# Three PSUM banks for the input projection during the recurrence of a hybrid decoder layer

## The chip, the cores and the metric

The kernel runs on one core of a Trainium2 chip. The metric is the device time of one execution in microseconds, as the median of several runs. Each kernel is also executed once under the hardware profiler; that execution has a time of its own, and the trace covers its span from the first to the last instruction.

The engines are TensorE (PE in the profile; its weight loads PEld), VectorE (DVE), ScalarE (ACT), GpSimd (POOL) and SyncE (SP), which issues the DMAs. TensorE writes its products to PSUM, eight banks of 128 x 512 float32; here ScalarE and VectorE read them out, and a bank can take a new product when the last reader of the old one is done.

## What is computed

One decoder layer for 1024 tokens of width 1024, float32. The part this change touches is the projection of the normed input and the RWKV-7 recurrence fed by it:

```
u = rmsnorm(h, mix_pre_norm)
z = u @ w_in                      # attention q,k,v | r,k,v,w,a,g of the recurrence | gates
# per head, 64 x 64 state, for every token t:
sa    = state @ a_t               # a_t = -kk
state = state * w_t + sa b_t^T + v_t k_t^T
y_t   = state @ r_t
```

Behind it come the normalisation of y, a causal attention over three dilated groups, a gated merge of both branches, an output projection, a squared-ReLU MLP with 4096 hidden columns, and a gated embedding, each with an RMSNorm.

## The kernel before

Every product of dense weights is done in three float32r products of a high and a low part (mm3, lines 289 to 297): L292 high by high, L294 and L296 the mixed ones. So a half of a projection (zhalf, line 348: one 128-column weight tile by 512 tokens) is 24 matmuls of 128x512 into one bank named z. Each weight tile is loaded raw (wr), split by ScalarE into its high part (wh) and by GpSimd into its low part (wl). One weight tile serves two halves, so two z banks in turn.

The recurrence is done in chunks of 64 tokens, for four units w of two heads each (128 channels). For a unit the steps are:

- elementwise (line 596): decays, the key norm (hs, rn, bc), then AR and BK, the scaled keys and receivers; then the products A of BK and AR, four tokens' chunks at a time, masked by VectorE into the tile TM.
- invert (690): the inverse of a triangular matrix per chunk. VectorE does 31 pairs of operations on xy and pt; they are put into its gaps. Then 32x32 transposes on VectorE (TN<-xy, TM<-xy) and two sets of 32 small products on TensorE, tq and tr, whose results ScalarE copies to TQ and TN.
- fold_v (747) and fold (772): vt and kv bring the values in; bt and at are transposes of BK and AR, fq, kx and wr are products that fold the inverse into one matrix and one vector per chunk.
- scan (828): 14 states in a row; each is one product q on TensorE and one operation AR<-q on VectorE.
- read_out (840) and post (862): y, its norm (hv, yt on TensorE; sq, yc, vc, rb on ScalarE and VectorE).

Between these small products TensorE works on halves of z: of the units' r, k and v, of the attention's q, k, v, and of the gates (16 tiles that no step waits for soon, which fill).

The program has no order that stands in the text. A planner (class Order, line 136) runs generators at build time: the chains of the recurrence when their modelled operands are ready, else the next matmul of a dense half. It records all instructions of an engine in the order in which it came to them, and each engine executes in that order. The planner has modelled durations of every engine, and for the banks of the chains a time until which each is busy: chain_bank (308) takes the bank of its tags that is free earliest and lets other work go ahead until then. For a bank of z it has no such time. What the chip waits for are the semaphores between writer and readers of a tile, and of a bank.

The eight banks carry the tags z0, z1, s0 to s3, m0, m1. z takes its banks in turn by a counter (zbank, 341). The chains before the change: m0 and m1 for most steps; s2 and s3 for A besides, and for y; s0 and s1 for at, kx and q.

Of the kernel before, what the change touches and what calls it, by code (L numbers as in the profile page):

```python
# [26 lines left out]
NU = RW // 128  # L27
# [217 lines left out]
def layer(ctx: ExitStack, tc: tile.TileContext, x, pT, wz, wup, w_out, wff1, w_ff2, w_ple, w_pleg,  # L245
# [26 lines left out]
    done = set()  # L272

    def mm(out_, a, b, us, start=True, stop=True):
        PE.matmul(out_, a, b, start=start, stop=stop)  # L275
        m = math.prod(a.shape[1:])
        sch.turn("full" if a.shape[0] > 64 and m > 64 else (a.shape[0], m))
        sch.t = max(sch.t, sch.written.since(a, None) - 0.1, sch.written.since(b, None) - 0.1) + us
        sch.written.put(out_, sch.t, None)
        sch.dep = sch.t  # L280

    def tr(out_, a, us, idn=None):
        PE.transpose(out_, a, ident if idn is None else idn)  # L283
        sch.turn("full" if a.shape[0] > 64 else a.shape[0])
        sch.t = max(sch.t, sch.written.since(a, None) - 0.1) + us
        sch.written.put(out_, sch.t, None)
        sch.dep = sch.t
# [20 lines left out]
    def chain_bank(shape, name, tags=("m0", "m1")):  # L308
        tag = sch.first(tags)
        yield from sch.free(tag)  # L310
        return psum.tile(shape, F32, name=name, tag=tag), tag
# [28 lines left out]

    def zbank():
        tags = ("z0", "z1", "s0")
        if ("X", 0) in done and ("P", NU - 1, 1) not in done:
            tags = tags[0:2]
        zn[0] += 1
        return psum.tile([128, 512], F32, name="z", tag=tags[zn[0] % len(tags)])

# [6 lines left out]
    with tc.tile_pool(name="xin", bufs=1) as xp:  # L354
# [19 lines left out]
        def keep_warm(n):  # L374
            keep = zbank()[:, 0:128]
            for i in range(n):
                mm(keep, one, one, 0.107)
# [3 lines left out]
        for b, c in enumerate((slice(0, 512), slice(512, 1024))):  # L381
            ps = psum.tile([128, 512], F32, name="gb", tag=f"s{b + 2}")
# [28 lines left out]
        def z_quarter(n, q):  # L411
            h, ts = q // 2, slice((q % 2) * 256, (q % 2) * 256 + 256)
            if q % 2 == 0:
                zl[h].append(psum.tile([128, 512], F32, name="z", tag="s3") if h and n else zbank())
            hi, lo = wl[n]
            now(mm3(zl[h][n][:, ts], [(hi[:, k * 128:k * 128 + 128], lo[:, k * 128:k * 128 + 128],
                                       uT[0][h][:, k, ts], uT[1][h][:, k, ts]) for k in range(KT)]))
# [63 lines left out]
    def add_z(wi, evac, gate=None):  # L481
        def body(hi, lo):
            for h in range(2):
                ps = zbank()
                yield from zhalf(ps, hi, lo, h)
                evac(h, ps)
        sch.add(body, lambda: wload(wz[wi]), gate)
# [25 lines left out]
    for h in range(2):  # L513
        for n, t in ((0, xw), (1, xg)):
            ps = zl[h][n]
# [256 lines left out]
    def fold(w):  # L772
        d = U[w]
        AR, BK, TM, TN, UV, wc = (d[n] for n in ("AR", "BK", "TM", "TN", "UV", "wc"))
        for b in range(4):
            ps, tag = yield from chain_bank([128, 4, 128], "bt")
            for i in range(4):
                tr(ps[:, i, :], BK[:, 4 * b + i, :], 0.11)
            S.activation(TM[:, 4 * b:4 * b + 4, 0], ps.rearrange("p c (h k) -> p c h k", h=2), AF.Copy)
            sch.hold(tag)  # L780
        t0 = sch.dep
        for b in range(2):
            ps, tag = yield from chain_bank([128, 4, 128], "at", ("s0", "s1"))
            for i in range(4):
                c = 8 * b + 2 * i
                tr(ps[:, i, :], AR[:, 0, c:c + 2].rearrange("p c t -> p (c t)"), 0.11)
            for i in range(2):
                S.activation(BK[0:64, 8 * b + i:8 * b + 8:2, :], ps[64 * i:64 * i + 64], AF.Copy)
            sch.hold(tag)
        yield sch.until(t0)  # L790
        for g in range(4):
            ps, tag = yield from chain_bank([128, 4, 128], "fq")
            for i in range(4):
                for h in range(2):
                    mm(ps[64 * h:64 * h + 64, i, :], TN[:, 2 * (4 * g + i) + h, :],
                       TM[0:64, 4 * g + i, :, h], 0.095)
            ps = ps.rearrange("p c (x t) -> p c x t", x=2)
            S.activation(TM[0:64, 4 * g:4 * g + 4, :, 0], ps[0:64], AF.Copy)
            V.tensor_copy(TM[0:64, 4 * g:4 * g + 4, :, 1], ps[64:128])
            sch.hold(tag)  # L800
        yield sch.until(sch.dep)
        for g in range(2):
            cg = slice(8 * g, 8 * g + 8)
            ps, tag = yield from chain_bank([128, 8, 64], "kx", ("s0", "s1"))
            for i in range(8):
                for h in range(2):
                    hp = slice(64 * h, 64 * h + 64)
                    mm(ps[hp, i, :], TM[:, 8 * g + i, 0, h], UV[:, 8 * g + i, hp], 0.06)
            V.tensor_tensor(AR[:, 0, cg], ps, wc[:, cg, None].to_broadcast([128, 8, 64]), OP.mult)
            sch.hold(tag)  # L810
        for g in range(4):
            cg = slice(4 * g, 4 * g + 4)
            ps, tag = yield from chain_bank([128, 4, 128], "wr")
            for i in range(4):
                for h in range(2):
                    hp = slice(64 * h, 64 * h + 64)
                    mm(ps[hp, i, :], BK[0:64, 4 * g + i, hp], TM[0:64, 4 * g + i, :, h], 0.095)
            for h in range(2):
                V.scalar_tensor_tensor(TM[:, cg, 0, h], ps[:, :, 0:64], hb[h],
                                       ident[:, None, 64 * h:64 * h + 64].to_broadcast([128, 4, 64]),  # L820
                                       op0=OP.mult, op1=OP.add)
            V.tensor_tensor(AR[:, 1, cg], ps[:, :, 64:128], AR[:, 1, cg], OP.add)
            sch.hold(tag)
        done.add(("F", w))
# [3 lines left out]
    def scan(w):  # L828
        d = U[w]
        AR, TM, wc = d["AR"], d["TM"], d["wc"]  # L830
        for c in range(1, NCH - 1):
            if c % 8 == 1:
                qb, tag = yield from chain_bank([128, 8, 64], "q", ("s0", "s1"))
            q = qb[:, (c - 1) % 8, :]
            mm(q, TM[:, c, 0].rearrange("p h k -> p (h k)"), AR[:, 0, c - 1], 0.113)
            V.scalar_tensor_tensor(AR[:, 0, c], q, wc[:, c:c + 1], AR[:, 0, c], op0=OP.mult, op1=OP.add)
            sch.hold(tag)
            yield None
# [73 lines left out]
    def rwkv():  # L912
        for w in range(NU):
            yield from fold_v(w)
            yield from wait(lambda: ("T", w) in done)
            yield from fold(w)
            yield from scan(w)
            yield from read_out(w)
# [752 lines left out]
    P = {}  # L1671
# [265 lines left out]
```

## Time and profile before

| | us |
|---|---|
| median of 3 runs | 1775.32 |
| lowest and highest run | 1775.20, 1776.92 |
| profiled execution | 1773.19 |
| its span, first to last instruction | 1771.4 |
| TensorE, time with a matmul under way | 1743.8 |
| VectorE busy | 1017.1 |
| ScalarE busy | 732.3 |
| GpSimd busy | 670.5 |

The stages in the trace: the load and norm of the input to about 57 us, the recurrence with its projections from there to about 490, the attention with the rest of the projections to about 824, then merge, output projection, MLP and embedding to the end.

How the lines are read. A timeline row has the start in us, the length, the engine, the line, the operation, what is written and read with its shapes, and how many instructions the row merges; in brackets how long the engine was idle before, and who ended that. Most operations of VectorE, ScalarE and GpSimd are recorded by one helper and show as L113, small products as L275, transposes on TensorE as L283, DMAs as L132; there the tile names tell them apart. A float32 product that is not float32r shows as two matmuls. A row of busy time by stage has the stretch, its length, then for PE, PEld, DVE, ACT and POOL the busy time and the number of instructions, then the granted TensorE clock as a share, the DMA engines' busy share and GB/s. A row of waits has the engine and its product, who ended the wait, the total in us, the number of times and the longest.

### The profile page before, as it was taken

To read this page: it belongs to the slowest core of one execution; us is meant where nothing else is said; L and a number is where in the kernel's file an instruction comes from. 1 tells how busy PE (TensorE), PEld (TensorE's weight loads), DVE (VectorE), ACT (ScalarE), POOL (GpSimd) and SP (SyncE) were. 2 spreads that over 40 slices of the span, in tenths; PEclk is the share of its full clock that TensorE was granted. 3 is DMA by queue.
4 is the path that set the end of the run, shared out by engine and by line. 5 is a ranking of instruction groups with operands and counts; after the bars stand their busy time and mean duration, and the time that the engine had idled before them with its cause. 6 is when DMAs were issued, how large, how long until landed. Compare 5 with 4: busy or idle time off the path is not lost.

```text
span 1771.4 us, 25935 instructions
## 1 busy us (share of the span) xinstructions
PE 1743.8 (98%) x10192; PEld 1423.4 (80%) x10192; DVE 1017.1 (57%) x1834; ACT 732.3 (41%) x1315; POOL 670.5 (38%) x423
## 2 busy tenths in 40 slices
PE   9999989999999999999999999999999999999998
PEld 8787877878877777778888878888788888888887
DVE  6289777776534233353735466665666566556643
ACT  5824343432344343542434434343334334333454
POOL 1344131231232323332230266666665566652311
PEclk9999999999999999999999999999999999999999
DMA  4621121212332222333524132332232232305611
GB/s 163 211 95 37 49 78 47 98 43 96 86 134 84 60 60 72 110 111 135 201 96 139 64 113 95 94 115 87 92 118 91 84 95 90 123 9 179 214 48 48
DMA packets 67132, 175.51 MB, mean 99 GB/s; under 512 B 7745, under 2 KB 8129, under 8 KB 66498
## 3 DMA queue, kind: packets, MB, share of 16 engines
q1 hardware_dynamic: 67010, 173.86, 29.6%
q8 instruction: 80, 1.31, 0.3%
q14 instruction: 42, 0.34, 0.1%
HBM read 125.20 MB, written 41.94 MB: 94 GB/s over the span
## 4 chain that ended last, share of the span: by engine, by line
PE 82%; DVE 5%; DMA 5%; ACT 3%; POOL 2%; issue 2%; SPq 0%; DVEq 0%; ACTq 0%; POOLq 0%
PE z L294 18%; PE z L296 18%; PE z L292 18%; PE bk L292 6%; PE bk L294 5%; PE bk L296 5%; PE sc L275 1%; DVE xy L113 1%; PE y L275 1%; PE po L275 1%; PE pt L283 1%; PE A L275 1%; PE wr L275 1%; PE fq L275 1%; POOL wl L113 1%
## 5 line engine op out<-in xcount | busy, mean ns | idle before, releaser
L113 POOL TENSOR_TENSOR wl<-wr,wh 128x1024 fp32r<-128x1024 f32 (+1 forms) x87 | 208.0, 2392 | 431.4 <-ACT wh L113 412.2
L113 DVE TENSOR_TENSOR tot<-tot,bk 128x512 f32<-128x512 f32 x420 | 272.7, 682 | 129.9 <-PE bk L296 129.7
L292 PE MATMUL z<-uh,wh 128*128 128x512 f32 (+1 forms) x800 | 312.3, 390 | 5.5 <-ACT part L113 3.0
L296 PE MATMUL z<-uh,wl 128*128 128x512 f32 (+1 forms) x800 | 312.6, 391 | 2.7 <-POOL wl L113 2.7
L294 PE MATMUL z<-ul,wh 128*128 128x512 f32 (+1 forms) x800 | 313.6, 392 | 1.3 <-DVE ul L113 1.3
L292 PE MATMUL z<-f,wh 128*128 128x512 f32 x496 | 193.2, 389 | 0.3 <-ACT f L113 0.3
L294 PE MATMUL z<-f,wh 128*128 128x512 f32 x496 | 193.1, 389 | 0.2 <-DVE f L113 0.2
L296 PE MATMUL z<-f,wl 128*128 128x512 f32 x496 | 193.0, 389 | 0.0
L292 PEld LDWEIGHTS z<-uh,wh 128*128 128x128 f32 x800 | 151.1, 189 | 36.2 <-ACT part L113 3.5
L296 PEld LDWEIGHTS z<-uh,wl 128*128 128x128 f32 x800 | 151.0, 189 | 34.1 <-POOL wl L113 4.0
L294 PEld LDWEIGHTS z<-ul,wh 128*128 128x128 f32 x800 | 151.2, 189 | 32.3 <-issue 3.6
L292 PE MATMUL bk<-duo 128*128 128x512 f32 x420 | 164.3, 391 | 4.0 <-DVE tot L113 3.9
L294 PE MATMUL bk<-duo 128*128 128x512 f32 x420 | 163.5, 389 | 0.0
L296 PE MATMUL bk<-duo 128*128 128x512 f32 x420 | 163.5, 389 | 0.0
L113 ACT ACTIVATE wh<-wr 128x1024 fp32r<-128x1024 f32 (+1 forms) x87 | 90.3, 1038 | 119.0 <-PE z L294 89.8
L113 POOL TENSOR_TENSOR duo<-w2r,duo 128x512 fp32r<-128x512 f32 x45 | 66.7, 1483 | 166.0 <-ACT duo L113 166.0
L113 POOL TENSOR_TENSOR duo<-ws,duo 128x512 fp32r<-128x512 f32 x60 | 81.0, 1350 | 122.3 <-ACT duo L113 119.0
L292 PEld LDWEIGHTS z<-f,wh 128*128 128x128 f32 x496 | 93.1, 188 | 20.0 <-ACT f L113 0.5
L294 PEld LDWEIGHTS z<-f,wh 128*128 128x128 f32 x496 | 93.1, 188 | 19.8 <-DVE f L113 0.5
L296 PEld LDWEIGHTS z<-f,wl 128*128 128x128 f32 x496 | 93.1, 188 | 19.2
L292 PEld LDWEIGHTS bk<-duo 128*128 128x128 f32 x420 | 78.8, 188 | 23.7 <-DVE tot L113 7.0
L296 PEld LDWEIGHTS bk<-duo 128*128 128x128 f32 x420 | 78.8, 188 | 16.4
(312 smaller groups left out, 3203.5 us busy)
## 6 DMA issues: line engine op xcount, KB each, us to landing
wr<-in_wz_dram SPq DMA_DIRECT2D x48, 512.0 KB, 3.7
wr<-in_wff_dram SPq DMA_DIRECT2D x31, 512.0 KB, 3.6
w2r<-in_w_ff_dram SPq DMA_DIRECT2D x30, 512.0 KB, 4.2
xt<-in_x_dram SPq DMA_DIRECT2D x16, 512.0 KB, 4.3
gscr<-gst SPq DMA_DIRECT2D x32, 256.0 KB, 2.0
g<-gscr SPq DMA_DIRECT2D x16, 512.0 KB, 4.2
wpg<-pkg SPq DMA_DIRECT2D x16, 512.0 KB, 6.7
sw<-qk SPq DMA_DIRECT2D x48, 128.0 KB, 2.3
```

The lines of the kernel that those rows point to most:

```text
L113: return f(*a, **kw)
L275: PE.matmul(out_, a, b, start=start, stop=stop)
L283: PE.transpose(out_, a, ident if idn is None else idn)
L292: PE.matmul(ps, ah, bh, start=start and i == 0, stop=False, skip_group_check=not start)
L294: PE.matmul(ps, ah, bl, start=False, stop=False, skip_group_check=not start)
L296: PE.matmul(ps, al, bh, start=False, stop=i == n - 1, skip_group_check=not start)
```

## The change

z takes three banks (z0, z1, s0) at all times; before, it took only two of them from the start of the recurrence until its last unit was done. In exchange the chains give up s0. The transposes at and the products kx may use s1, m0 or m1, whichever is free earliest; the states q of the scan use s1 alone.

```
     def zbank():
         tags = ("z0", "z1", "s0")
-        if ("X", 0) in done and ("P", NU - 1, 1) not in done:
-            tags = tags[0:2]
         zn[0] += 1
         return psum.tile([128, 512], F32, name="z", tag=tags[zn[0] % len(tags)])
...
-            ps, tag = yield from chain_bank([128, 4, 128], "at", ("s0", "s1"))
+            ps, tag = yield from chain_bank([128, 4, 128], "at", ("s1", "m0", "m1"))
...
-            ps, tag = yield from chain_bank([128, 8, 64], "kx", ("s0", "s1"))
+            ps, tag = yield from chain_bank([128, 8, 64], "kx", ("s1", "m0", "m1"))
...
-                qb, tag = yield from chain_bank([128, 8, 64], "q", ("s0", "s1"))
+                qb, tag = yield from chain_bank([128, 8, 64], "q", ("s1",))
```

The planner sees other banks for the chains, and from the first folding on, at about 182 us of the trace before, it comes to another order, on all engines, until the end of the attention. The matmuls are the same 8637 in both programs.

The largest move that the prediction speaks of is at the second unit's inverse (w = 1). On TensorE there, the products tq and tr before:

```order
L275 MATMUL A<-AR,BK 128x128 x8
L275 MATMUL tq<-TN,TM 32x32 x32
L294 MATMUL z<-ul_128,wh 128x512
...
L275 MATMUL A<-AR,BK 128x128 x8
...
L275 MATMUL A<-AR,BK 128x128 x8
...
L275 MATMUL tr<-TQ,TM 32x32 x32
L296 MATMUL z<-uh_127,wl 128x512
L283 MATMUL bt<-cs,BK 128x128 x4
```

and with the change:

```order
L275 MATMUL tq<-TN,TM 32x32 x32
L292 MATMUL z<-uh_127,wh 128x512
L275 MATMUL hv<-cs,sq 128x2 x4
L294 MATMUL z<-ul_129,wh 128x512
L296 MATMUL z<-uh_127,wl 128x512
L292 MATMUL z<-uh_127,wh 128x512
L275 MATMUL tr<-TQ,TM 32x32 x16
L294 MATMUL z<-ul_129,wh 128x512
L275 MATMUL tr<-TQ,TM 32x32 x16
```

The products A of the third unit, which stood before, between and behind, now come after bt and at; four z matmuls and one hv are left between tq and the first tr, where 16 z and two groups of A stood. Ahead of tq there are now 15 z matmuls, two half groups of bc and kv since vt; before there were 42 z besides bc, kv, hv, two groups of A and yt.

On VectorE, what stands between the two transposes that tq and tr read, before:

```order
L113 STREAM_TRANSPOSE TN<-xy 32x32x32
L113 TENSOR_TENSOR TM<-A,cs 128x8x64 x2
L113 SCALAR_TENSOR_TENSOR yc<-yc,pr,yt 128x512
L113 TENSOR_TENSOR yc<-yc,bv 128x512
L113 SCALAR_TENSOR_TENSOR og<-yc,pr,og 128x512
L113 STREAM_TRANSPOSE TM<-xy 32x32x16x2
```

and with the change:

```order
L113 STREAM_TRANSPOSE TN<-xy 32x32x32
L113 COPY UV<-kv 64x8x64
L113 SCALAR_TENSOR_TENSOR kk<-k,pr,bc 128x512
L113 SCALAR_TENSOR_TENSOR AR<-kk,Ep 128x16x63
L113 TENSOR_SCALAR AR<-kk 128x16
L113 TENSOR_TENSOR BK<-BK,En 128x16x64
L113 STREAM_TRANSPOSE TM<-xy 32x32x16x2
L113 STREAM_TRANSPOSE TN<-xy 32x32x32
L113 TENSOR_TENSOR BK<-BK,kk 128x16x64
L113 RECIPROCAL vc<-vc 128x8
```

The third unit's elementwise steps, which were done before the first transpose, now stand between the two, and the reciprocal of the first unit's norm stands behind both.

On ScalarE, a little earlier, the high part wh of a weight has moved ahead of the third unit's key norm. Before:

```order
L113 ACTIVATE BK<-a,oka,pr 128x16x64
L113 ACT_TABLE_LOAD
L113 ACTIVATE rn<-rn 128x16
L113 ACTIVATE kk<-rn 128x512 x2
L113 ACT_TABLE_LOAD
L113 ACTIVATE En<-Ep 128x1024
L113 ACTIVATE Ep<-Ep 128x1024
L113 ACTIVATE wh<-wr 128x1024
```

and with the change:

```order
L113 ACTIVATE BK<-a,oka,pr 128x16x64
L113 ACTIVATE wh<-wr 128x1024
L113 ACT_TABLE_LOAD
L113 ACTIVATE rn<-rn 128x16
L113 ACTIVATE kk<-rn 128x512 x2
L113 ACT_TABLE_LOAD
L113 ACTIVATE En<-Ep 128x1024
L113 ACTIVATE Ep<-Ep 128x1024
```

GpSimd's low part of the same weight moves with it. Behind the products tq and tr, ScalarE's copies of tr (TN<-tr) now stand after vc and rb of the first unit's norm, and rb reads the reciprocal named above.

## The prediction

> **What bounds the kernel now.** I read the page first, then busy time by stage, then TensorE's waits, then the instructions in order of time at the two places the waits name.
>
> ```profile
> span 1771.4 us, 25935 instructions
> PE 1743.8 (98%) x10192; PEld 1423.4 (80%) x10192; DVE 1017.1 (57%) x1834; ACT 732.3 (41%) x1315; POOL 670.5 (38%) x423
> ```
>
> TensorE is busy for 98% of the span, and the change neither adds nor removes a matmul. What it can win is idle time of TensorE, in the stages where it acts: from 146 us to the early attention at 560.
>
> ```profile
> 146.00:152.00 6.00, 2.69 (x15) 1.99 (x16) 4.80 (x12) 5.94 (x9) 2.81 (x2) 1.00 0.02 5
> 152.00:155.40 3.40, 3.40 (x10) 2.63 (x9) 3.40 (x3) 1.47 (x2) 3.40 (x5) 0.50 0.00 0
> ...
> 182.00:262.00 80.00, 75.38 (x708) 61.14 (x704) 60.54 (x126) 29.60 (x43) 20.10 (x15) 1.00 0.19 63
> 262.00:330.00 68.00, 67.06 (x742) 54.80 (x740) 49.73 (x98) 21.66 (x36) 12.72 (x13) 1.00 0.22 75
> 330.00:490.00 160.00, 158.88 (x1489) 130.95 (x1488) 106.83 (x202) 60.13 (x90) 42.41 (x25) 1.00 0.25 80
> 490.00:560.00 70.00, 67.92 (x488) 52.45 (x486) 32.06 (x97) 32.77 (x84) 18.46 (x8) 1.00 0.33 110
> ```
>
> Length minus the first busy column is TensorE's idle time: 3.31, 0, 4.62, 0.94, 1.12 and 2.08 us, 12.1 in all (from 155.4 to 182 it never idled). The second row also ran at a granted clock of 0.50. More than these 12.1 us and the slow clock cannot be won. Who ended the waits between 140 and 490 us:
>
> ```profile
> PE z L292 <- ACT part L113: 3.0, 1, 3.0
> PE z L296 <- POOL wl L113: 1.5, 1, 1.5
> PE A L275 <- ACT yc L113: 1.2, 1, 1.2
> PE z L292 <- ACT gst L113: 1.0, 1, 1.0
> ```
>
> The first and the last are z products that wait until ScalarE has emptied an old z bank: two waits, 4.0 us. These a third bank can remove.
>
> **Place one, 148 to 164 us (the same order before and after).**
>
> ```profile
> 146.28 1.18 PE L283 MATMUL bc<-cs,kk 128*128 128x128 f32 x8 [0.36 <-ACT kk L113]
> ...
> 147.99 0.40 PE L296 MATMUL z<-uh,wl 128*128 128x512 f32 x1
> ...
> 150.68 0.68 ACT L113 ACTIVATE part<-z,pr 128x512 f32<-128x512 f32 x1
> ...
> 151.42 0.50 PE L292 MATMUL z<-uh,wh 128*128 128x512 f32 x1 [3.03 <-ACT part L113]
> ...
> 156.10 0.39 PE L294 MATMUL z<-ul,wh 128*128 128x512 f32 x1
> 156.32 0.39 PE L296 MATMUL z<-uh,wl 128*128 128x512 f32 x1
> ...
> 163.37 0.39 PE L292 MATMUL z<-uh,wh 128*128 128x512 f32 x1
> 163.69 2.06 PE L275 MATMUL A<-AR,BK 64*128 64x128 f32 x32
> ```
>
> The z half that starts at 151.42 is the 13th z tile of the kernel's counter; with two tags it takes the bank of the 11th, whose second copy (part) ends at about 151.3. With three it takes the bank of the 10th, emptied a projection earlier. So the wait goes: 151.42 - 147.99 = 3.43, less the normal step of 0.23 (156.10 to 156.32), is 3.20 us. The 13 matmuls from 151.42 to 156.10 took 4.68 against 13 x 0.23 = 2.99: the slow clock cost another 1.7. TensorE would reach the decay products A at 163.69 - 3.20 - 1.7 = 158.8.
>
> But A reads BK, and VectorE is the one late next:
>
> ```profile
> 151.50 2.50 POOL L113 TENSOR_TENSOR AR<-r,Ep 128x1024 f32<-128x1024 f32 x1
> 151.79 2.35 DVE L113 TENSOR_TENSOR xy<-xy,pt 64x112 f32<-64x112 f32 x1
> 154.06 1.39 DVE L113 SCALAR_TENSOR_TENSOR kk<-k,pr,bc 128x512 f32<-128x512 f32 x2
> 155.48 2.01 DVE L113 SCALAR_TENSOR_TENSOR AR<-kk,Ep 128x1008 f32<-128x1008 f32 x1
> 157.41 2.37 DVE L113 TENSOR_SCALAR AR<-kk 128x16 f32<-128x16 f32 x1
> 159.69 1.21 DVE L113 TENSOR_TENSOR BK<-BK,En 128x1024 f32<-128x1024 f32 x1
> 161.76 1.21 DVE L113 TENSOR_TENSOR BK<-BK,kk 128x1024 f32<-128x1024 f32 x1
> ```
>
> VectorE runs without a gap from 151.79 to 162.97 and waits for nothing of TensorE's there (its last input of TensorE's, bc, ended at 147.5). BK is done at 161.76 + 1.21 = 163.0 whether or not z waited. So A starts at 163.0 instead of 163.69: the stall moves from the z bank to A, about 4.2 us long, and the gain is 0.7. After an idle stretch of 3.03 us TensorE ran 3.4 us at half clock; if 4.2 us of idling does the same, 1.7 are lost again behind A. Bounds -0.7 and +1.0; the 1.0 + 1.5 us of idling around 228 us did not slow the clock, so I take the middle, +0.2. [...]
>
> **Place two, the second unit's inverse (in the trace 218 to 275 us).** Two waits go: z for gst (1.0), and wl (1.5), since the split of that weight (wh on ScalarE) now stands ahead of the third unit's key norm instead of behind its exponentials. The planner also moves the third unit's A and the first unit's yt behind the inverse, so the wait A <- yc (1.2) goes. Together the idle time there is the 4.62 above. What comes instead: the second inverse's products tq and tr now stand close together. Between them stood 16 z and two A, now 4 z and one hv (four products).
>
> ```profile
> 239.77 2.05 PE L275 MATMUL vt<-cen,v 128*128 128x128 f32 x16
> ...
> 244.98 2.08 PE L275 MATMUL kv<-UV,TM 64*64 64x64 f32 x64
> 251.65 1.05 PE L275 MATMUL hv<-cs,sq 128*128 128x2 f32 x8 [0.93 <-DVE UV L113]
> ...
> 261.15 2.21 PE L275 MATMUL tq<-TN,TM 32*32 32x32 f32 x64
> ...
> 269.80 2.21 PE L275 MATMUL tr<-TQ,TM 32*32 32x32 f32 x64
> ```
>
> Before, tq to tr took 8.65; now 2.21 + 4 x 0.23 + 1.05 = 4.2. In that time VectorE must finish the transpose TM<-xy, which stands behind the third unit's elementwise steps:
>
> ```profile
> 242.49 0.69 DVE L113 COPY UV<-vt 64x512 f32<-64x512 f32 x1 [0.20 <-ACT UV L113]
> ...
> 243.62 2.40 POOL L113 TENSOR_TENSOR wl<-wr,wh 128x1024 fp32r<-128x1024 f32 x1 [14.28 <-ACT wh L113]
> ...
> 245.96 3.37 POOL L113 TENSOR_TENSOR AR<-r,Ep 128x1024 f32<-128x1024 f32 x1
> ...
> 247.00 2.38 DVE L113 TENSOR_SCALAR AR<-kk 128x16 f32<-128x16 f32 x1
> ...
> 253.70 2.20 DVE L113 STREAM_TRANSPOSE TN<-xy 32x1024 f32<-32x1024 f32 x1
> ...
> 259.42 1.94 DVE L113 STREAM_TRANSPOSE TM<-xy 32x1024 f32<-32x1024 f32 x1
> ...
> 373.29 0.17 DVE L113 TENSOR_SCALAR AR<-kk 128x16 f32<-128x16 f32 x1
> ```
>
> I count from the end of vt on TensorE (239.77 + 2.05 = 241.8; VectorE's copy of it ends at 243.18, 1.4 later). Its work up to tq (15 z at 0.23, bc 1.2, kv 2.1) is 6.7, up to tr 10.9. VectorE: UV<-vt is done at 1.4; the last steps of the inverse, half of kk and half of UV<-kv bring it to 4.4, TN<-xy to 6.6 (just in time for tq); then UV 0.69, kk 0.7, AR up to 2.0, the small AR 0.17 (373.29, where GpSimd was idle), BK 1.21, TM<-xy 1.94: 13.3. So tr waits about 2.4. Behind it ScalarE's copies of tr now stand behind rb, which needs a reciprocal that stands on VectorE behind the second transpose (2.2) and BK (1.2); bt needs the banks of tr. That puts bt about 2.9 late in all. This is the lower bound. The upper one: GpSimd's wl and AR run at just this time, and where they meet VectorE's operations on SBUF (247.00: 2.38 for the same 16 elements) each costs up to a whole GpSimd operation; with both (2.40 and 2.50, less what overlaps the waits above) bt is about 6.0 late, and the denser fold behind it (wr with single z between, on three VectorE operations each) may add up to 2. So 2.9 to 8.0 replaces 4.62: -1.7 to +3.4. One collision is what the trace has at each of these places (157.41, 247.00), 2.2 us; I take 2.9 + 2.2 - 4.6 = +0.5.
>
> **The rest.** (a) The banks. The transposes at, products kx and states q leave s0. q keeps one bank: its ninth state waits for the release of the eighth, which its own data already waits for: 0, covered by the chain AR -> q -> AR. at and kx share m0 and m1 with bt, fq and wr; the planner knows this and puts z between, so it is an order matter. (b) The order has 6806 rows for 6798 on TensorE. A change between z and a small product costs about 0.1 each way (163.69 needed 0.32 from the z before, not 0.23), so up to 8 x 0.2 = +1.6; counting neighbours by kind I find between -1.4 and +0.6; taken as 0. (c) From 262 to 560 us other steps meet: 4.1 us of idling are there (0.94, 1.12, 2.08). They may vanish or double; nothing favours either: 0. The halves of z behind the recurrence already rotate over three banks.
>
> **Sum.** +0.2 + 0.5 + 0 + 0 = +0.7 on the profiled execution's 1773.19 (span 1771.4), so 1773.9. The median of the runs is 1775.32, 2.1 above it; the forecast is 1776.0.
>
> **Rivals.** *The waits simply go* (faster): VectorE catches up, as it has idle time of 19 us between 182 and 262 (80 - 60.54), and the planner's order holds. For it: the z waits are real, 3.0 and 1.0, with 1.7 of slow clock. Against: A's operand does not come earlier. With 0.7 at place one, half of the 4.6 and half of the 4.1, minus 1.4 from neighbours: -6.4, so 1769. If place one gave all 4.9 as well it would be 1765. *VectorE is shut out at the second inverse* (slower): GpSimd's wl and AR both come first, tr and bt are 8.0 late (+3.4), and such a stall brings the half clock (+1.7 at one place or the other): +5.1, so 1780.5. It decides from the second collision on. [...] *The change does not do what it says*: z never meets a full bank more than twice in this stage, so the third bank is idle and only the replanned order is measured; the sum is then (b) and (c) alone, 1775, hardly to be told from the forecast.
>
> **How the numbers follow.** This kernel's measurement can tell about 0.2%, 3.5 us. Forecast (moved waits, within 3.5 us) 0.46 and the last rival 0.04, together 0.50 for no change; waits go 0.27; shut out 0.23. The likeliest case alone spans 1772 to 1779; with the others reaching in, 1769 to 1781.5.
>
> **What would show it.** The z waits for part and gst are gone; A near 159 us waits about 4 us for VectorE's BK; tq or tr of the second inverse waits for VectorE 2 us or more; TensorE's idle time from 146 to 560 stays between 9 and 16 us. Wrong: A starts before 162, or idle time under 6 or over 18 us.

## The result, and the profile after

The changed kernel took 1792.5 us (median of four runs, 1791.0 to 1793.1), the kernel before beside it 1776.1 (1775.2 to 1777.0): a ratio of 1.0089, 95% interval 1.0073 to 1.0105. It is 16 us slower; the forecast was 1776.0 and its range ended at 1781.5. Over all runs on record the difference is somewhat smaller, 13.2 us of span (table below). One run of the kernel before, in a slow state (span 1923.3 us at a mean clock of 0.849), is left out here and everywhere below.

First the head of the page of the changed kernel, then busy time by stage in the stretches used before (length, TensorE, its weight loads, VectorE, ScalarE, GpSimd, and then the granted clock of TensorE):

```profile
span 1789.2 us, 25954 instructions
PE 1757.5 (98%) x10192; PEld 1435.0 (80%) x10192; DVE 1025.5 (57%) x1834; ACT 731.6 (41%) x1315; POOL 666.1 (37%) x423
```

```profile
146.00:152.00 6.00, 5.62 (x29) 4.70 (x30) 4.79 (x12) 5.94 (x9) 2.70 (x2) 1.00 0.02 5
...
155.40:182.00 26.60, 22.27 (x244) 18.55 (x243) 23.39 (x25) 6.08 (x10) 8.78 (x7) 0.87 0.18 61
182.00:262.00 80.00, 75.93 (x754) 61.44 (x753) 62.84 (x123) 30.50 (x45) 17.83 (x14) 0.93 0.15 50
262.00:330.00 68.00, 67.01 (x615) 54.28 (x614) 41.62 (x82) 17.79 (x29) 12.33 (x11) 0.96 0.27 90
330.00:490.00 160.00, 156.62 (x1497) 128.14 (x1496) 112.77 (x209) 60.44 (x93) 35.06 (x24) 0.96 0.19 64
490.00:560.00 70.00, 67.81 (x469) 54.19 (x468) 29.40 (x72) 28.51 (x59) 21.27 (x8) 1.00 0.39 118
560.00:800.00 240.00, 238.20 (x1369) 184.18 (x1368) 96.34 (x293) 107.34 (x246) 73.68 (x30) 1.00 0.28 82
```

Two things are to be seen. TensorE's idle time (length minus its busy time) from 146 to 560 us is 0.38 + 0 + 4.33 + 4.07 + 0.99 + 3.38 + 2.19 = 15.3 us, where it was 12.1; with the 1.80 of the last row (0.14 before) the idle time has grown by 4.9. But the span has grown by 17.8, with the same number of matmuls. The rest is in the clock column, where before all of these stretches but one of 3.4 us read 1.00. The granted clock stood at 0.50 in five places; the same view, for exactly these:

```profile
162.16:168.99 6.83, 5.73 (x37) 5.14 (x38) 6.49 (x9) 0.60 (x1) 0.00 (x0) 0.50 0.00 0
247.49:254.32 6.83, 5.73 (x29) 4.40 (x30) 6.73 (x8) 0.00 (x0) 1.14 (x2) 0.50 0.10 39
257.73:267.97 10.24, 10.24 (x83) 8.34 (x82) 2.02 (x3) 2.65 (x6) 0.00 (x0) 0.50 0.01 2
356.72:360.13 3.41, 3.41 (x9) 2.64 (x8) 3.13 (x4) 2.90 (x5) 2.36 (x1) 0.50 0.66 210
455.71:465.95 10.24, 10.24 (x88) 8.58 (x88) 3.86 (x4) 3.91 (x6) 1.13 (x1) 0.50 0.47 130
```

That is 37.5 us at half clock against 3.4. Every length is a multiple of 3.41 us (once, twice or three times), and so are the distances of the starts from the first (85.33, 95.57, 194.56 and 293.55 us are 25, 28, 57 and 86 times 3.413): one grid of windows. The 34.1 us more can cost at most half, 17.1; 17.8 - 4.9 = 12.9 of it shows.

The two page heads give the same account without a subtraction of that kind. Over the whole span TensorE idled 1771.4 - 1743.8 = 27.6 us before and 1789.2 - 1757.5 = 31.7 after, 4.1 more. In its half-clock windows it was busy for 3.40 us before (the row 152.00:155.40) and for 35.35 after (the five rows above). With half of that taken off, the busy time is 1742.1 before and 1739.8 after: nearly the same work. So of the 17.8 us, 4.1 are idling and at most 16.0 are half clock; the 2.3 too many are in part small products, which lose less than half (32 rows of tr took 1.91 us at 258.10, at half clock, and 1.19 at 175.85, at full clock).

The five longest waits of TensorE between 140 and 490 us:

```profile
PE A L275 <- DVE pt L113: 4.3, 1, 4.3
PE bc L283 <- DVE UV L113: 3.1, 1, 3.1
PE q L275 <- DVE AR L113: 2.6, 4, 0.8
PE hs L275 <- ACT kk L113: 1.1, 1, 1.1
PE tq L275 <- DVE vc L113: 0.9, 1, 0.9
```

No z product waits for part or gst any more: the change does what it says. At place one its stall stands where the prediction put it:

```profile
158.54 0.39 PE L292 MATMUL z<-uh,wh 128*128 128x512 f32 x1
163.26 3.15 PE L275 MATMUL A<-AR,BK 64*128 64x128 f32 x26 [4.33 <-DVE pt L113]
```

(VectorE's last step of BK ended at 163.1; the view names the instruction beside it.) The A products took 3.15 us for the 26 rows shown (3.79 for all 32) where 32 rows took 2.06 before: the half clock came in behind the wait, and stayed for two windows, 6.83 us. The second group of A, behind the same matmuls in both kernels, started at 170.40 instead of 168.17: in this execution place one cost 2.2 us, more than the prediction's bound of +1.0, which had one window of half clock in it. Place two (in the trace before 218 to 275 us) is different from the forecast; TensorE, VectorE (with the same two steps of the unit before, at 163 us) and GpSimd there, in order of time:

```profile
239.26 2.05 PE L275 MATMUL vt<-cen,v 128*128 128x128 f32 x16
...
244.34 1.15 PE L275 MATMUL kv<-UV,TM 64*64 64x64 f32 x32
248.59 1.11 PE L283 MATMUL bc<-cs,kk 128*128 128x128 f32 x4 [3.10 <-DVE UV L113]
253.47 2.54 PE L275 MATMUL tq<-TN,TM 32*32 32x32 f32 x64
256.28 0.95 PE L275 MATMUL hv<-cs,sq 128*128 128x2 f32 x8
258.10 1.91 PE L275 MATMUL tr<-TQ,TM 32*32 32x32 f32 x32
```

```profile
163.04 0.18 DVE L113 TENSOR_TENSOR pt<-xy,Mp 64x31 f32<-64x31 f32 x1
163.25 0.18 DVE L113 TENSOR_TENSOR xy<-xy,pt 64x31 f32<-64x31 f32 x1
...
243.85 1.66 DVE L113 TENSOR_TENSOR pt<-xy,Mp 64x31 f32<-64x31 f32 x1
245.55 2.26 DVE L113 TENSOR_TENSOR xy<-xy,pt 64x31 f32<-64x31 f32 x1
247.84 0.69 DVE L113 COPY UV<-kv 64x512 f32<-64x512 f32 x1
...
254.48 1.91 DVE L113 STREAM_TRANSPOSE TM<-xy 32x1024 f32<-32x1024 f32 x1
```

```profile
243.10 2.37 POOL L113 TENSOR_TENSOR wl<-wr,wh 128x1024 fp32r<-128x1024 f32 x1 [11.07 <-ACT wh L113]
245.41 2.35 POOL L113 TENSOR_TENSOR AR<-r,Ep 128x1024 f32<-128x1024 f32 x1
```

The last pair of the inverse's steps took 1.66 and 2.26 us; at 163 us, with GpSimd idle (the row 162.16:168.99 above), it took 0.18 each. Each ends (245.51 and 247.81) when one of GpSimd's two operations does (245.47 and 247.76). VectorE's copy of kv is late by that, and bc needs kv's bank: 3.10 us. Neither tq nor tr of this inverse waits then. VectorE was done with the second transpose at 254.48 + 1.91 = 256.39 us, 15.1 after the end of vt (239.26 + 2.05 = 241.31) where the prediction had 13.3; but TensorE reached tr only 16.8 after it, where the prediction had 10.9: the 3.1 at bc and about 2.9 lost in the half clock from 247.49 to 254.32 are the difference.

### The profile page after: what moved, and what is told of

Its sections match the earlier page's. It is cut to its first block, busy times and chain, and to the rows that moved or that the text cites. A ratio compares the mean times of both kernels' runs of the same rounds, so it can differ in the third digit from the quotient of the medians.

```text
span 1789.2 us, 25954 instructions
## 1 busy us (share of the span) xinstructions
PE 1757.5 (98%) x10192; PEld 1435.0 (80%) x10192; DVE 1025.5 (57%) x1834; ACT 731.6 (41%) x1315; POOL 666.1 (37%) x423
## 4 chain that ended last, share of the span: by engine, by line
PE 80%; DVE 8%; DMA 5%; ACT 4%; POOL 2%; issue 1%; SPq 0%; DVEq 0%; ACTq 0%; POOLq 0%
PE z L294 17%; PE z L296 17%; PE z L292 17%; PE bk L292 6%; PE bk L294 5%; PE bk L296 5%; DVE xy L113 2%; DVE pt L113 1%; PE sc L275 1%; PE po L275 1%; PE A L275 1%; PE pt L283 1%; PE wr L275 1%; PE tp L283 1%; DMA g<-gscr 1%
```

## How much the clock varies from run to run

Each run lists its span and mean granted clock. The runs of the kernels that matter most, pooled (span, not time; 1.8 us less than the time; the last kernel also has z's third bank at place one):

```
kernel                            runs  mean span (standard error)  lowest to highest  mean clock
before                              74  1775.5 (0.3)                1768.4 to 1780.0   0.9949
changed                             15  1788.7 (0.7)                1784.3 to 1791.6   0.9890
its order, z on two banks           10  1785.2 (0.8)                1782.5 to 1791.5   0.9916
at alone moved                      10  1781.6 (1.3)                1776.2 to 1790.0   0.9923
kx alone moved                      12  1778.7 (0.8)                1774.1 to 1785.7   0.9922
z's third bank at place one only    10  1776.4 (1.0)                1771.5 to 1780.8   0.9949
changed, waits covered               6  1786.2 (1.5)                1783.3 to 1792.4   0.9938
before, waits covered               10  1772.3 (0.3)                1770.1 to 1773.9   0.9982
```

The 74 runs of one program scatter over 11.6 us, and the clock goes with them: a straight line through them (span against mean clock) has 1768.1 us at a clock of 1.000 and 1.43 us more for each 0.001 below. The changed kernel's 15 runs give 1772.4 and 1.48. So of 13.2 us between the means, 0.0059 of clock at 1.45 is 8.6, and 4.6 would be left at full clock, close to the 4.9 of added idle time in the profile. The profiled execution of the kernel before had one half-clock stretch in the recurrence; its mean run had more (0.0051 x 1775.5 x 2 = 18 us at half clock, about 2 of it at the program's end, where the profiled executions of the two kernels had 1.5 and 2.3). The changed kernel's three profiled executions had 37.5, 37.5 and 27.3 us at half clock before 800 us, and its mean run has about 37 by the same sum (0.0110 x 1788.7 x 2 = 39, 2 of it at the end): the profile of the kernel before, with its 3.4, is the one that was far from its mean.

## Experiment 1: what makes the half clock

A kernel that leaves the layer out and runs products alone: z products, and between them each of the kernel's small products back to back, then mixtures, then waits for chains of ScalarE operations of growing length.

```diff
+    dense(60)
+    for f, n in ((tq, 540), (kv, 540), (bt, 150), (A, 260), (fq, 260), (kx, 360), (vt, 130), (hv, 130)):
+        f(n)
+        dense(27)
+    for k in (1, 2, 4, 8):
+        for i in range(round(18 / (0.6 + 0.2267 * k))):
+            tq(16)
+            dense(0.2267 * k)
+        dense(27)
+    for m in (1, 2, 3, 4, 5, 6, 8, 4, 3, 5, 2, 6):
...
```

> The layer is left out: TensorE runs z products (128x512) with stretches between them of one kind of small product alone, back to back: tq, kv, bt, A, fq, kx, vt and hv shapes, about 18 us of each at the durations of the profile before; then tq groups of 16 with 1, 2, 4 or 8 z between; then waits for ScalarE of growing length. Theory 1 (only idling lowers the clock): granted clock 1.00 through all the stretches of products, and 3.4 us at 0.50 behind each wait of 3 us or more. Theory 2 (small products count for little, idle or not): the clock falls to 0.50 inside the 18 us of tq (540 at 0.0345) and kv, with no idling, comes back in the z stretch behind them, and stays at 1.00 for vt and bt.

Busy time and clock by stretch (here without a VectorE column: length, TensorE, weight loads, ScalarE, GpSimd, clock). The stretches are tq's first window, the rest of tq, kv, hv's first window, the rest of hv, then tq groups with 1, 2 and 4 z between:

```profile
67.49:70.90 3.41, 3.41 (x108) 3.41 (x108) 0.00 (x0) 0.00 (x0) 1.00 0.02 5
71.10:122.80 51.70, 51.70 (x972) 51.67 (x969) 0.00 (x0) 0.00 (x0) 0.50 0.01 2
151.40:183.00 31.60, 31.60 (x1081) 31.54 (x1080) 0.00 (x0) 0.00 (x0) 1.00 0.02 4
...
469.80:473.20 3.40, 3.40 (x32) 3.36 (x30) 0.00 (x0) 0.00 (x0) 1.00 0.02 5
474.00:521.80 47.80, 47.80 (x226) 47.80 (x225) 0.00 (x0) 0.00 (x0) 0.50 0.00 0
555.71:600.00 44.29, 44.29 (x580) 35.77 (x576) 0.00 (x0) 0.00 (x0) 0.50 0.01 2
637.70:680.00 42.30, 42.30 (x478) 32.66 (x477) 0.00 (x0) 0.00 (x0) 0.50 0.01 1
```

```profile
707.70:728.00 20.30, 20.30 (x327) 15.85 (x327) 0.00 (x0) 0.00 (x0) 1.00 0.01 2
```

TensorE was never idle in these rows. The 32x32 products halved the clock after one window and held it down to their end; so did the products with two columns (hv). kv (64x64, 31.6 us), bt (16.5 us), A (29.2), fq (28.5), kx (21.1) and vt (29.1) ran at 1.00 throughout. tq with one or two z for each 16 fell to 0.50, with four it stayed at 1.00. So theory 2 (small products count for little) holds for tq and not for kv, and theory 1 (only idling lowers the clock) falls. Its 3 us fall too, by two waits of the same length:

```profile
832.19:835.60 3.41, 1.33 (x7) 0.79 (x6) 1.86 (x3) 0.00 (x0) 1.00 0.00 0
835.61:839.00 3.39, 3.39 (x10) 2.61 (x9) 0.00 (x0) 0.00 (x0) 0.50 0.03 5
1091.61:1095.02 3.41, 1.58 (x7) 0.97 (x6) 1.66 (x3) 0.00 (x0) 1.00 0.00 0
1095.05:1098.40 3.35, 3.14 (x14) 2.60 (x15) 0.16 (x1) 0.00 (x0) 1.00 0.00 0
```

TensorE idled 2.08 us in the first window and 1.83 in the third (of a wait of 2.07, the rest of which fell into the next window). The first was followed by half clock, the other was not.

One measure puts both kinds together: give each product its rows times columns as a share of 128x128, the largest that the rows show (below, the array), for the time its moving columns need (0.2267 us for z's 512 float32r columns, the step from one z to the next at full clock, 0.44 ns a column; each of the records of a plain float32 product counts twice as long per column, as vt's 128x128 in the probe, which took 29.2 us for 260 of them, 0.112 each, 0.88 ns a column), and add up per window of 3.41 us. In the 18 traces of this study, away from the start and the end of the programs, there are 8526 windows at full clock. Of 47 whose sum is below 0.30, 46 were followed by half clock; of 84 between 0.30 and 0.42, 16; of the 8395 above, none. At half clock a window holds about half as many products (z's step was 0.43 us from 249.93 to 252.91 in the changed kernel, 0.23 at full clock), and there 86 of 86 windows below 0.33 stayed, 59 of 59 above 0.42 left, and of some 13 between the two about 10 stayed. The bounds were set on these same windows, not tried on others. In the changed kernel the windows ahead of the five stretches had 0.01, 0.15, 0.26, 0.08 and 0.10. The third of them (254.3 to 257.7) was busy all the time, in part with the tq and hv quoted above. The two waits of 2.1 us above had 0.31 and 0.42 in the first of their windows, close to the bounds. Which counter the chip uses is not shown by this; that the sum separates the windows is.

## Experiment 2: the order and the banks apart

The order of the change, z on two banks in the recurrence as before:

```diff
     def zbank():
         tags = ("z0", "z1", "s0")
+        if ("X", 0) in done and ("P", NU - 1, 1) not in done:
+            tags = tags[0:2]
```

> The three changed lists of banks of the change (at, kx, q), with z on two banks in the recurrence as before: the order is the changed kernel's, row for row. If the order costs the time: 1789 to 1796 us and the same half-clock stretches (30 us or more of them after 240 us). If the third z bank does it: 1773 to 1778.

1786.1 us, ratio 1.0050 (1.0031 to 1.0069): most of the loss without the third bank. It lies between the two cases of the expectation, and its profiled execution had 10.2 us at half clock between 240 and 560 us, not 30 or more (a later execution, below, 23.9). The changed kernel once more:

> The changed kernel once more, beside the others of this call. The spans of the kernel before lay on 1767.6 us at a granted clock of 1.000 and 1.4 to 1.5 us more for each 0.001 below it. If the changed kernel has the same slope: about 1773 us at full clock and 1786 to 1794 as it runs, with 30 to 45 us at half clock; if its first four runs were a chance: 1778 to 1785.

1790.0, ratio 1.0064 (1.0044 to 1.0084).

Both kernels again, side by side:

> The changed kernel beside the same order on two z banks (next run), in one call. If the third bank of z adds to what the order costs: 3 to 5 us above it (so far 1787 to 1793 against 1785 to 1788, but in different calls). If the order alone makes the loss: within 1.5 us of it.

> The order of the change on two z banks, once more. With the third bank z does not wait at 148 and TensorE waits at A instead, 4.3 us; with two the wait of 3.2 us is at z. If the banks add: 1785 to 1787, mean granted clock 0.992 to 0.993, the changed kernel's 0.988 to 0.990. If the order alone: like the changed kernel, 1788 to 1792.

1791.3 with three banks, ratio 1.0077 (1.0061 to 1.0093); 1786.8 with two, ratio 1.0057 (1.0041 to 1.0074). The intervals overlap; over all runs it is 1788.7 to 1785.2 of span, 3.5 us with a standard error of about 1.1, and the clock is 0.9890 to 0.9916, worth 3.8. The third bank itself probably costs some of the loss. Why is open: with two banks TensorE waits for z (3.0 and 1.7 us) instead of A, and its later steps come earlier (VectorE's copy of kv at 246.47 instead of 247.84), so that they may meet the windows otherwise, but no run takes that apart.

Of the moved products, q alone leaves the order as it was, row for row, when the program is built; no run was made of it. The other two, each alone:

```diff
-            ps, tag = yield from chain_bank([128, 4, 128], "at", ("s0", "s1"))
+            ps, tag = yield from chain_bank([128, 4, 128], "at", ("s1", "m0", "m1"))
```

> The kernel before with only the transposes at moved to s1, m0, m1: another order again (1672 rows of difference to before on TensorE), banks of z as before. If the time hangs on what the order does to the clock, not on the banks: the span above 1771.4 is about 0.39 us for each us at half clock above before's 3.4 (13.3 us for 34.1 us in the changed kernel), plus the change of idling. If moving the chain products to m0 and m1 costs by itself: between 1780 and 1790 without more half clock.

> The kernel before with only the key products kx moved to s1, m0, m1 (the states q alone leave the order as it is, row for row). If each replanned order costs by its own waits and half clock: span about 1768 at full clock plus its added waits, plus 1.45 us for each 0.001 of clock; between 1774 and 1790, with waits of the changed kernel's kind (bc for VectorE's UV, hs, tq) where the order is the changed one. If the at part alone (1783) makes the loss: 1776 to 1779.

at alone: 1783.1, ratio 1.0036 (1.0018 to 1.0054). kx alone: 1780.4, ratio 1.0018 (1.0007 to 1.0029). Both orders are slower than the old one; by the clock of their runs (0.9923 and 0.9922) some 4 us are half clock in each, which leaves 2 to 3 for at and nothing for kx.

## Experiment 3: place one alone

Two kernels missed the place. The wait at 151.42 is the 21st z tile's, not the 13th's as the prediction counted; and the A products there are the second unit's, not the first's.

> The kernel before with the third z bank kept until the first unit's A is issued: the order is that of before, row for row, and only place one (148 to 164 us) changes. By the prediction's working the z wait of 3.2 us goes and A waits about 4 us for BK: -0.7 to +1.0, so 1775 to 1776.5. If the half clock follows such a wait as it does in the changed kernel (6.8 us at 0.50 from 162): about 1777 to 1779. If the waits simply went: 1770.

> The kernel before, order row for row, with one z half alone (the 13th z tile, at 151.42) in s0 instead of z1. By the prediction's working of place one: no wait of 3.2 us there, A waits about 4.2 us and starts near 163.0; between -0.7 and +1.0 us. By the share of the array that is filled per 3.41 us (0.05 to 0.37 of it before half clock in the runs so far): 1.3 half-clock stretches of 3.41 us behind A instead of 0.8 behind z, so the same within 1 us. If a z wait is worth its length: -3.

Both have the order of before and still z's wait of 3.0 us: 1776.0 each, ratios 0.9995 (0.9981 to 1.0009) and 1.0000 (0.9987 to 1.0013). They serve as repeats of the kernel before: their profiled executions had 13.7 us at half clock in the recurrence, at 150 and 263, where that of before had 3.4. The third kernel:

```diff
-        return psum.tile([128, 512], F32, name="z", tag=tags[zn[0] % len(tags)])
+        return psum.tile([128, 512], F32, name="z", tag="s0" if zn[0] == 21 else tags[zn[0] % len(tags)])
```

> z_early and z_place left the z wait of place one as it was (their third bank went to other z tiles; it is the 21st tile of the counter that waits at 151.42). The kernel before, order row for row, with that tile alone in s0 instead of z1. By the prediction's working: no wait of 3.2 us, A waits about 4.2 us and starts near 163.0; -0.7 to +1.0 us. By the share of the array filled per 3.41 us: about 1.3 half-clock stretches behind A instead of about 0.9 at z: the same within 1 us, 1775 to 1777.5. If a z wait is worth its length: -3, 1773.

TensorE at place one in this kernel:

```profile
158.87 0.39 PE L292 MATMUL z<-uh,wh 128*128 128x512 f32 x1
163.68 2.72 PE L275 MATMUL A<-AR,BK 64*128 64x128 f32 x23 [4.43 <-DVE pt L113]
```

1778.6, ratio 1.0003 (0.9986 to 1.0019). The wait went from z to A, and nothing was won; in its profile one window of half clock followed, not two. That is the prediction's reading of this place. The interval is -2.5 to +3.4 us; it leaves out a gain of 3, what the z wait is long, but cannot tell the +0.2 from its bounds of -0.7 and +1.0.

## Experiment 4: products in the waits

If half clock comes from windows with little in them, products that add nothing should prevent it where TensorE waits anyway. nil is a tile of zeros; cover(n) adds n z products with zero weights to the z bank in work, with no time in the planner, so the order stays. The four calls stand ahead of the products A, bc, hs, and each group of tq and of tr.

```diff
+    def cover(n):
+        for i in range(n if zcur[0] is not None else 0):
+            PE.matmul(zcur[0], nil, uT[0][0][:, 0, :], start=False, stop=False)
...
+            cover(17 if w == 1 and g == 0 else 0)
+            cover(12 if w == 2 and hs.start == 0 else 0)
+        cover(6 if w == 3 else 0)
+            cover(3 if w in (1, 3) else 0)
```

> The changed kernel in its order, with 59 z products more that add nothing (zero weights, 13.4 us of TensorE's time at 0.2267): 17 before the second unit's A, 12 before the third unit's bc, 6 before the fourth unit's hs, 3 before each of the tq and tr groups of the second and fourth units. If the half clock makes the loss: the stretches at 162, 247 to 268, 356 and 455 go or shrink to a third, and the kernel is faster with more work, 1780 to 1786. If the waits and the order make it, and the clock only follows: the added work in the waits is hidden and the rest comes on top, 1793 to 1800.

> after_cover again with its zero weights made by GpSimd, not by ScalarE in the first turn (where the making moved everything behind it by about 3.7 us). 59 z products of 0.2267 are 13.4 us; 8.4 of it lies in waits of 4.3, 3.1, 1.1 and 0.7 us, 5.0 comes on top. If the half clock costs 1400 to 1500 us times the part of the clock that is missing (0.0113 in the changed kernel's runs, 0.0033 expected here): 1772 + 5 + 5 = 1782 of span, 1784 us, some 5 below the changed kernel with more work in it. If the half clock costs nothing by itself: 1793.

The first, 1791.2, ratio 1.0081 (1.0060 to 1.0103), also had its whole program moved by the making of nil in the first turn, and tells little. The second is 1791.1, ratio 1.0078 (1.0052 to 1.0103). The clock did what was expected, 0.9963; the time did not. Its trace shows why. The 59 products are 13.4 us of work, but TensorE's idle time over the span fell only from 31.7 to 28.8 us (1788.5 - 1759.7), so about 10.5 of them came on top, not 5.0; and the time at half clock before 800 us, 10.2 instead of 37.5, gave back about as much, at most 12.6. With covers only in the waits (17, 12 and 5 products):

> The changed kernel with z products of zero weights only where TensorE waits (17 before the second unit's A, 12 before the third unit's bc, 5 before the fourth unit's hs: 7.7 us of work in 8.5 us of waiting), none at tq and tr. If half clock costs time that waits would not take anyway: the stretches at 162, 247 and 356 go and the kernel is 3 to 5 us faster than the changed one. If TensorE then only waits longer elsewhere (for VectorE at tr, for ScalarE at yt, as in after_cover_2): the same within 1.5 us.

1786.4, ratio 1.0061 (1.0043 to 1.0078), beside 1.0077 (1.0061 to 1.0093) of the changed kernel. The clock rose from 0.9890 to 0.9938, worth 7 us by the slope, and the mean span fell by 2.5 (standard error 1.6). In the profiled execution the stretches at 162 and 356 were gone, but 17.1 us at half clock were left, 10.2 of them from 251.6 on, over hv and tr. Where part of the rest went is in TensorE's waits from 140 to 560 us:

```profile
PE q L275 <- DVE AR L113: 4.9, 6, 1.3
PE tr L275 <- DVE TM L113: 1.9, 1, 1.9
PE yt L283 <- ACT rb L113: 1.8, 1, 1.8
PE bc L283 <- DVE UV L113: 0.6, 1, 0.6
PE A L275 <- DVE pt L113: 0.5, 1, 0.5
```

The covered waits are 0.6 and 0.5 instead of 3.1 and 4.3, but tr now waits 1.9 where it waited 0.3, and q 4.9 where it waited 3.4 in this stretch. Over the whole span the 34 products, 7.7 us, took only 5.3 us of idle time away (31.7 to 26.4). TensorE, less slowed, came earlier to the places where it needs VectorE and ScalarE. So in this order part of the half clock stands in for waits, and the slope of the runs overstates what could be won back.

> The changed kernel with a pause of 1.3 us in the planner between the two tq groups and between the two tr groups of each inverse, so that z stands between them; no work added, another order. If dense small products and waits make the half clock: no half clock at tq and tr (257 to 268 and 455 to 466 in the changed kernel), the one behind A at 162 stays; 1776 to 1784. If the change's loss is in its waits and its order by themselves: 1787 to 1793.

```diff
+            if b:
+                yield 1.3
             ps, tag = yield from chain_bank([128, 16, 32], "tq")
...
+            if b:
+                yield 1.3
             ps, tag = yield from chain_bank([128, 16, 32], "tr")
```

1792.6, ratio 1.0094 (1.0062 to 1.0126). In its profile, of the fastest of its four runs (1785.7; the others 1790.4 to 1796.4), no tq or tr ran at half clock, and 13.7 us were left in all in the recurrence, but this order has waits of its own from 130 to 560 us (q 3.9, z for wl 3.7, hs 2.4 and 1.1, tq 1.4, hv 1.2, beside the 4.3 at A): here spreading small products in the planner gave for waits what it took from half clock.

On the kernel before, with place one's bank moved:

> z_place with 24 z products more that add nothing (zero weights): 17 before the second unit's A, 5 before the third unit's second group of A (which waits 1.17 for yc), 2 between the second unit's tq groups. If the half clock costs about 1.35 us for each 3.41 us: no half clock from 147 to 167 and from 257 to 268, 2 to 4 us faster than before. If not: 0 to +1.

> z_place_2 with 24 z products of zero weights (17 before the second unit's A, 5 before the third unit's second group of A, 2 between the second unit's tq groups), the weights made by GpSimd. All but 0.5 us of the added work lies in waits. If the half clock costs 1.35 us for each 3.41 us: about two of before's four expected stretches go, 1772 to 1774.5. If not: 1776 to 1778.

The first missed place one like z_place and had its start moved: 1780.6, ratio 1.0020 (1.0006 to 1.0033). The second is 1774.0, ratio 0.9981 (0.9971 to 0.9991), with the head of its page and TensorE at place one:

```profile
span 1772.2 us, 25984 instructions
PE 1747.6 (99%) x10216; PEld 1427.6 (81%) x10216; DVE 1017.6 (57%) x1834; ACT 731.9 (41%) x1315; POOL 668.4 (38%) x424
```

```profile
158.88 4.06 PE L361 MATMUL z<-uh,nil 128*128 128x512 f32 x17
163.47 2.06 PE L275 MATMUL A<-AR,BK 64*128 64x128 f32 x32 [0.53 <-DVE pt L113]
```

A starts when BK is done, as ever, but runs its 32 rows in 2.06 us. No half clock was granted in its profiled execution before 1770 us, and over ten runs the mean span is 3.2 us under the kernel before, and 4.1 under the same kernel without the 24 products (1776.4); the clock, 0.9982 for 0.9949, is worth 4.7 of that by the slope. The ten runs scatter over 3.8 us, where ten runs of each of the three kernels of experiment 3 scatter over 7.2 to 9.3. It is faster than both kernels, by doing 24 products more.

## Why the prediction was wrong, by its steps

- **What bounds.** TensorE's idle time and its clock were named as the only things to win. That held, but they were taken from one execution. Its one slow stretch of 3.4 us was read as what the kernel has; the mean run has four to five times that. What could be lost was never asked: the 12.1 us are a limit for a gain and not for a loss.
- **Place one.** The wait was read rightly: the stall moved from z (3.03) to A (4.33), A started at 163.26 against 163.0, and alone the move changes the time by a ratio of 1.0003. The half clock behind it was not: two windows instead of at most one, so that the profiled execution lost 2.2 us here. The count of the z tile was wrong, which has no effect on the sum; and the row 157.41, 2.37 us for 128x16, ran beside GpSimd's wl of 3.36 us and ended with it (159.78 and 159.75).
- **Place two.** The idle time there was taken to grow by 0.5; it went from 4.62 to 4.07. That the two are near each other is luck, for the place in it was wrong: not tr waits (0 instead of about 2.4) but bc, earlier, because GpSimd's wl and AR met the last two steps of the inverse (1.66 and 2.26 us, where 0.18 each was taken beside an idle GpSimd); TensorE, held up there and slowed by the clock, was later at tr than VectorE. The rival of VectorE shut out had this mechanism, with two collisions as its condition; the trace shows both. Its price, 1780.5, was still 12 us short.
- **The rest, (c).** 4.1 us of idling from 262 to 560 became 6.6, and 0.14 became 1.80 behind it. Together that cost 4.1 where 0 was taken; "they may vanish or double" was written of the first alone, and it kept to that.
- **The step that failed: the half clock.** It was sized as 1.7 us at one place, as a follower of an idle stretch of 3 us or more ("the 1.0 + 1.5 us of idling around 228 us did not slow the clock, so I take the middle"). In the traces it went with how much of the array was used per 3.41 us (below 0.30, 46 of 47 windows were followed by it; above 0.42, none of 8395), so tq, tr and hv with 4 z between counted nearly as idling (0.26 in the window from 254.3), and the prediction itself had shown that these were packed together. Priced by that, the order change was worth 34 us more at half clock in the profiled run and 21 in the mean (0.0059 x 1788.7 x 2), 9 us in the mean and 13 in the profiled run instead of 0 to 1.7. With 4.1 to 4.9 us more of idling this accounts for the whole difference, where the prediction's sum had +0.7 for both together. It is not what could be won back: the kernel with products in this order's waits alone gained 2.5 us (standard error 1.6), in part because other waits came in their place.
- **What would show it.** Three of four signs came true (no z waits, A waits 4.3, idle time 15.3 within 9 to 16; tq and tr did not wait), with the time 16 us off. The signs tested the waits and not the clock.

## What to carry to other kernels

When an order packs small products together, add up the array's use per window as well as the waits: in these traces 46 of 47 windows of 3.41 us below 0.30 were followed by half clock, one of them (0.26) with TensorE busy all the time, and at half clock 86 of 86 below 0.33 stayed there. On the kernel before, 24 zero-weight products in waits that could not be avoided kept the clock (0.9982 for 0.9949), with 4.1 us less of mean span, and narrowed the scatter of the runs from 9.3 to 3.8 us; in the changed kernel 34 of them took off 2.5 (standard error 1.6), for there the other engines were not ready behind the waits (tr then waited 1.9 us for VectorE). Before a loss or gain of some microseconds is priced, look at a dozen runs with their clocks: the one profiled execution of the kernel before had 3.4 us at half clock in the recurrence, its mean run, by its clock, about 16.

## What was not expected of the hardware

TensorE at 100% busy lost half its clock: 3.41 us of 32x32 products alone were enough (67.49 to 70.90 in the probe), and 128x2 products did the same (469.80 to 473.20), while 64x64 products for 31.6 us did not. A wait of 2.08 us that fell whole into one window was followed by half clock, and one of 2.07 us that fell into two, 1.83 of it into the first, was not. Products with zero weights held the clock up like others: behind 17 of them, 4.06 us, the 32 rows of A took 2.06 us, where 23 rows took 2.72 without them. And executions of one program differed by 11.6 us of span over 74 runs, with the clock as the measure that tells them apart (1.43 us for each 0.001).
